# z of a forgetting-attention layer: from inside the attention loop to a stage of its own, by seven half-size products

## The chip, the cores and the metric

One core of one Trainium2 chip runs the whole step. The metric is device time in microseconds of one execution; the time of a kernel is the median of its runs.

## What is computed

Two layers over 640 tokens: 512 of a prompt and 8 x 16 new ones ("samples"), width 1024, inner width 2048. Layer 0 is a gated MLP, layer 1 an attention with 16 heads of 128 in which each head's output is gated:

```python
proj = h @ w_in                              # layer 1: q, k, v, z, each 2048 wide, and 16 forget logits
s = einsum(q, k) * scale + c_i - c_j         # c: running sum of log_sigmoid(forget logit)
p = softmax(where(key <= query, s, -inf))    # prompt: 512 keys; samples: 256 cached and 16 new keys
out = (einsum(p, v) * silu(z)) @ w_out
```

Both layers end with a norm, a residual and a gated per-layer embedding (the "tail"). k, v and the log forget values are outputs too. All data is fp32.

## The kernel before

A product in fp32 accuracy is made of three matmuls (`mm3`): each operand is split into a rounded part and a rest (`split`: ScalarE writes the rounded part, VectorE the rest), and high x high, high x rest, rest x high add up in one PSUM bank. So every weight is fetched (`fetch`, DMAs issued by SP, 512 KB a unit, into three or four buffers `RAW`), split into the ring `W` (`prefetch`), and used by `weights(n)`. Units come in the order of the list `units`. The activations `h` of all 640 tokens lie split in `A` (`h_hi`, `h_lo`).

Layer 0 makes its two gates u and z by `seven_products`: a 256-channel by 1024 by 640-token product is cut in two along each axis, and seven half-size products (four steps of 128 x 128 x 320 columns by `mm3`, 84 matmuls) take the place of eight (96 matmuls of 384 or 256 columns in layer 1). It costs sums: of the weights on GpSimd (`left_operands`, four of 512 elements a pair), of the activations once on VectorE (`right_operands`), and seven additions out of PSUM a pair on VectorE.

Layer 1 works on pairs of heads. `project(p, parts)` makes v, k, q and z of pair p, as generators that yield after each few matmuls how long they took (in nominal steps). `interleave(steps, pieces)` runs these steps and calls pieces of the attention of the pair before at given times: `prompt_pieces` (scores, `turn`, that is, transposes of the probabilities, and value products, four blocks a head) and `sample_pieces`. So TensorE's long projections cover the softmax on VectorE and ScalarE. The loop runs p = 0 to 6: project pair p + 1, attend pair p. At p = 6, z of pair 7 is left out of the loop and made after it, and the attention of pair 7 lies beside that z and the first output products of the `tail`. y of each pair goes to DRAM (`y_sc`) and is read back in the tail.

The order within an engine is set by the tile framework: it takes the program as written and re-orders the instructions of each engine by its own timeline. Each engine then runs its list in order; all DMAs but one are issued by SP, one after the other.

Of the kernel before, what the change touches and what calls it, by code (L numbers as in the profile page):

```python
# [56 lines left out]
def hybrid_trunk(tc, x_prompt, x_sample, ck, cv, clf, p_prompt, p_sample, norm_pre, norm_post,  # L58
# [27 lines left out]
    c_sc = dram.tile([H, SEQ], F32, name="c_sc")  # L86
    cs_sc = dram.tile([P, 272], F32, name="cs_sc")
    rs_sc = dram.tile([16, P], F32, name="rs_sc")

    def r1(o, n, p=P):  # L90
        return R1[:p, o:o + n]
# [62 lines left out]
    for p in range(8):  # L154
        for part in (2, 1, 0, 3):
            for kk in range(2):
                u_rows(f_win[0], kk * 512, part * E + p * 256, 4, 256)
    u_tail(f_wout, 1)
# [3 lines left out]
    S0, S1 = 16, 48  # L162
    SEVEN = (0, 2)
    items = []
    for i in range(len(units)):
        if not S0 <= i < S1 or i % 4 - i % 2 not in SEVEN:
            items.append((i, None))
        elif i % 2 == 0:
            items += [(i, j) for j in range(4)]

    n0 = S1 + 16 + 2 + 8
    few = range(n0, n0 + 64 + 12)
    place, last_use = [], [-1] * (2 * NW)
    state = {"raw": 0, "used": 0}

    def raw_of(i):
        if S0 <= i < S1:
            z = (i - S0 + 1) % 4
            if z == NRAW:
                return r1(o_X, 1024)  # L180
        else:
            z = i % NRAW if i < S0 else (i + 1) % NRAW
        return RAW[:, z * 1024:z * 1024 + 1024]
# [7 lines left out]
    def left_operands(i, j):  # L191

        (a11, a21), (a12, a22) = ([raw_of(r).rearrange("p (k n) -> p k n", k=4)[:, :, z:z + P] for z in (0, P)] for r in (i, i + 1))
        s2, s3, s1, s4 = (SF[:, z * 512:z * 512 + 512].rearrange("p (k n) -> p k n", k=4) for z in range(4))
        if j == 0:
            for o, a, b, op in ((s1, a21, a22, ALU.add), (s2, s1, a11, ALU.subtract), (s3, a11, a21, ALU.subtract),
                                (s4, a12, s2, ALU.subtract)):
                nc.gpsimd.tensor_tensor(out=o, in0=a, in1=b, op=op)
        return (a11, SF[:, :1024], SF[:, 1024:2048], raw_of(i + 1))[j]

    def prefetch(upto, i0=0):

        while len(place) < min(upto, len(items)):
# [13 lines left out]
            if j is None:  # L217
                split(hi, lo, raw_of(u))
            else:
                split(*((x.rearrange("p (k n) -> p k n", k=4) for x in (hi, lo)) if j == 0 else (hi, lo)), left_operands(u, j))  # L220
                if u > S0:
                    fetch(u + 4)
# [84 lines left out]
    def channel_steps(ws, hh, banks, splits=SPLITS):  # L307

        out = [bank(banks), bank(banks)]
        for k in range(8):  # L310
            w = [z[:, k % 4, hh * P:(hh + 1) * P] for z in ws[k // 4]]
            for (a, b), o in zip(splits, out):
                mm3(o[:, :b - a], w, h_at(k, a, b), k == 0, k == 7)
            yield 0.9
        return out
# [69 lines left out]
    o_X, o_ln, o_sum, o_th = 14208, 15232, 16256, 17216  # L385
# [4 lines left out]
    SF = pool2.tile([P, 2560], F32, name="sf")  # L390

# [6 lines left out]
    b11, b12, b21, b22, t_a, t_b = (r1(10240 + z * 1280, 1280).rearrange("p (k n) -> p k n", k=4) for z in (0, 1, 2, 3, 4, 0))  # L398

    def right_operands():  # L400

# [3 lines left out]
        for o, a, b, dst in ((t_a, b12, b11, 0), (t_b, b22, t_a, 1), (b21, b21, t_b, 2), (b12, b22, b12, None)):  # L405
            nc.vector.tensor_tensor(out=o, in0=a, in1=b, op=ALU.subtract)
            if dst is not None:
                split(*right_sum(dst), o)

# [24 lines left out]
    for p in range(4):  # L434
# [4 lines left out]
        for kk in range(4):  # L439
# [20 lines left out]
    fetch(S0 + 4)  # L460
# [25 lines left out]
    assert o_A + 256 <= o_X  # L486
# [63 lines left out]

    def eight_products(done):
        wz = weights(2)
        for i in range(2):
            for j, o in enumerate(channel_unit(wz, i, UZ)):
                done(i, j, o[:, :HT])
# [32 lines left out]
    for g in range(0, 16, 2):  # L588
        for part, finish in ((0, finish_u), (1, finish_z)):
            if 2 * part in SEVEN:  # L590
                seven_products(lambda i, j: uv_of(g + i)[part][:, HALF[j]], lambda i, j, c: finish(g, i, j, c))
            else:
                eight_products(lambda i, j, c: finish(g, i, j, c))
# [138 lines left out]
    pool2, R2 = second("r2b", F32)  # L732


    o = 0
    def tmpa(n, p=P):
        nonlocal o
        res = r2(o, n, p)
        o += n
        return res  # L740
# [22 lines left out]
    assert o <= 7168  # L763
# [314 lines left out]
    def y_again(g, half):  # L1078
# [3 lines left out]
        if half == 0 and 7 <= g < 11:  # L1082
            return f(A[:, 7680 + (g - 7) * TOK:7680 + (g - 6) * TOK])
        return r1(g * TOK, TOK) if g < 7 else r2((g - 7) * TOK, TOK)
# [5 lines left out]
    PARTS = (project_v, project_k, project_q, project_z)  # L1090
    interleave(project(0, PARTS), [(0.0, forget_logits), (6.0, log_forget), (20.0, forget_sums), (30.0, lambda: load_k(0, 0))])
    for p in range(7):
        length, step = (57, 5.6) if p < 6 else (43, 4.2)
        pieces = kv_times(p, 0, 5) + kv_times(p, 1, length / 2) + sample_times(p, 0, 5) + sample_times(p, 1, length / 2)
        pieces += [(2, lambda p=p: load_k(p, 1)), (length / 2 - 3, lambda p=p: load_k(p + 1, 0))]
        for hh in range(2):
            pieces += prompt_times(2 * p + hh, 2 + 4 * step * hh, step)
        interleave(project(p + 1, PARTS if p < 6 else PARTS[:3]), pieces)
        store_y(p)


# [43 lines left out]
```

## Time and profile before

| | |
|---|---|
| runs | 1334.85, 1336.32, 1334.9 us; median 1334.9 |
| profiled execution | 1334.83 us, span 1333.0 us |
| TensorE matmul busy | 1321.0 us (99% of the span) |
| VectorE, ScalarE, GpSimd busy | 766.4, 542.9, 135.7 us |
| granted TensorE clock, mean | 0.999 |
| DMA | 172.87 MB, 130 GB/s over the span |

Matmuls are pipelined: a matmul of 320 columns is shown as 310 ns, but the next one starts about 147 ns later. So what one costs is read from start to start, and a stretch of TensorE from the first start of one part to the first start of the next. `L249` to `L251` are the three lines of `mm3`, `L263` and `L264` the two of `split`, `L198` the weight sums, `L528` the additions of the seven products, `L583` a gate product, `L960` value products, `L953` transposes of probabilities, `L955` their copy out of PSUM, `L992` the transposes of the cached keys, `L406` a sum of `right_operands`. PE is TensorE, DVE VectorE, ACT ScalarE, POOL GpSimd.

### The profile page before, as it was taken

How to read it: one execution, taken by the hardware profiler on the slowest of the kernel's cores; microseconds unless marked ns; L12 is line 12 of the kernel's file. 1: busy time of each engine (PE TensorE's matmuls, PEld its weight loads, DVE VectorE, ACT ScalarE, POOL GpSimd, SP SyncE). 2: the span in 40 equal slices, each digit the busy share in tenths (PEclk: the TensorE clock that was granted, in tenths of full speed). 3: DMA queues.
4: the chain of work that ended last, by engine and by line, in shares of the span. 5: the costliest groups of instructions: out<-in, count | busy, mean ns of one | idle time of the engine just before them, and what ended most of it. 6: DMA issues, size and time to landing. Idle time of an engine off the chain costs nothing.

```text
span 1333.0 us, 21550 instructions
## 1 busy us (share of the span) xinstructions
PE 1321.0 (99%) x8363; PEld 1191.6 (89%) x8363; DVE 766.4 (57%) x1581; ACT 542.9 (41%) x1025; POOL 135.7 (10%) x144
## 2 busy tenths in 40 slices
PE   9999999999999999999999999999999999999998
PEld 6888999999988788999999999999999998888786
DVE  7744899998844546544545454444545465544642
ACT  5434555444535334523433333433334344435341
POOL 1013444543000100000000000000000000000100
PEclk9999999999999999999999999999999999999999
DMA  6432334232324204688778575778778687243211
GB/s 224 138 100 70 120 114 130 66 109 68 127 95 158 78 18 127 178 142 158 138 154 176 145 163 141 164 144 163 125 151 169 152 212 235 101 149 111 64 64 47
DMA packets 299913, 172.87 MB, mean 130 GB/s; under 512 B 188769, under 2 KB 269201, under 8 KB 299810
## 3 DMA queue, kind: packets, MB, share of 16 engines
q1 hardware_dynamic: 299666, 171.23, 51.7%
q8 instruction: 65, 1.06, 0.3%
q14 instruction: 38, 0.31, 0.1%
q10 hardware_dynamic: 144, 0.26, 0.1%
HBM read 149.86 MB, written 21.59 MB: 129 GB/s over the span
## 4 chain that ended last, share of the span: by engine, by line
PE 94%; DVE 3%; issue 1%; ACT 1%; DMA 0%; POOL 0%; SPq 0%; DVEq 0%
PE pb L249 28%; PE pb L251 27%; PE pb L250 27%; PE pb L960 3%; PE pb L953 1%; PE pb L1014 1%; PE pb L1040 1%; PE pb L287 1%; DVE W L264 1%; PE pb L565 1%; PE pb L1037 1%; DVE R L583 0%; DMA RAW<-in_gmlp_w_in 0%; PE pb L1032 0%; DVE R L528 0%
## 5 line engine op out<-in xcount | busy, mean ns | idle before, releaser
L249 PE MATMUL pb<-A,W 128*128 128x384 f32 (+2 forms) x1024 | 330.2, 322 | 2.1 <-DVE R L538 1.8
L251 PE MATMUL pb<-A,W 128*128 128x384 f32 (+2 forms) x1024 | 317.1, 310 | 0.0
L250 PE MATMUL pb<-A,W 128*128 128x384 f32 (+2 forms) x1024 | 316.6, 309 | 0.0
L249 PE MATMUL pb<-W,A 128*128 128x512 f32 (+1 forms) x840 | 298.3, 355 | 2.1 <-ACT R L686 1.4
L251 PE MATMUL pb<-W,A 128*128 128x512 f32 (+1 forms) x840 | 293.7, 351 | 0.6 <-DVE A L264 0.6
L250 PE MATMUL pb<-W,A 128*128 128x512 f32 (+1 forms) x840 | 294.0, 350 | 0.0
L264 DVE TENSOR_TENSOR W<-RAW,W 128x1024 fp32r<-128x1024 f32 (+1 forms) x156 | 194.0, 1244 | 139.7 <-ACT W L263 137.5
L263 ACT ACTIVATE W<-RAW 128x1024 fp32r<-128x1024 f32 (+1 forms) x156 | 161.1, 1033 | 156.8 <-PE pb L250 65.1
L249 PEld LDWEIGHTS pb<-A,W 128*128 128x128 f32 x1024 | 193.0, 188 | 10.9 <-issue 6.8
L250 PEld LDWEIGHTS pb<-A,W 128*128 128x128 f32 x1024 | 193.0, 189 | 0.6
L251 PEld LDWEIGHTS pb<-A,W 128*128 128x128 f32 x1024 | 192.6, 188 | 0.4 <-issue 0.4
L249 PEld LDWEIGHTS pb<-W,A 128*128 128x128 f32 x840 | 159.1, 189 | 26.4 <-issue 3.1
L251 PEld LDWEIGHTS pb<-W,A 128*128 128x128 f32 x840 | 158.9, 189 | 21.1 <-DVE A L264 0.9
L250 PEld LDWEIGHTS pb<-W,A 128*128 128x128 f32 x840 | 159.0, 189 | 20.4 <-issue 0.4
L264 DVE TENSOR_TENSOR A<-R,A 128x640 fp32r<-128x640 f32 (+1 forms) x51 | 41.0, 835 | 74.1 <-ACT A L263 71.9
L992 DVE STREAM_TRANSPOSE r2b_t<-r2b_t 128x256 f32<-128x256 f32 x128 | 46.4, 413 | 33.9 <-PE pb L1014 26.2
L263 ACT ACTIVATE A<-R 128x640 fp32r<-128x640 f32 (+1 forms) x51 | 36.6, 746 | 67.7 <-PE pb L250 65.7
L249 PE MATMUL pb<-tb,W 128*128 128x320 f32 x192 | 59.8, 312 | 0.1
L251 PE MATMUL pb<-tb,W 128*128 128x320 f32 x192 | 59.5, 310 | 0.0
L250 PE MATMUL pb<-tb,W 128*128 128x320 f32 x192 | 59.5, 310 | 0.0
L273 POOL TENSOR_TENSOR SML<-SML 128x1 f32<-128x1 f32 x25 | 18.1, 724 | 385.1 <-DVE SML L271 380.5
L955 ACT ACTIVATE R<-pb 128x128 f32<-128x128 f32 (+1 forms) x64 | 27.9, 436 | 65.7 <-PE pb L953 65.4
(235 smaller groups left out, 1866.7 us busy)
## 6 DMA issues: line engine op xcount, KB each, us to landing
RAW<-in_fox_w_in SPq DMA_DIRECT2D x64, 512.0 KB
RAW<-in_gmlp_w_in SPq DMA_DIRECT2D x40, 512.0 KB
r2b_t<-in_cache_fox_v SPq DMA_DIRECT2D x32, 512.0 KB
r2b_t<-in_cache_fox_k SPq DMA_DIRECT2D x128, 128.0 KB
RAW<-in_gmlp_w_out SPq DMA_DIRECT2D x16, 512.0 KB
RAW<-in_ple_w_gate SPq DMA_DIRECT2D x16, 512.0 KB
RAW<-in_fox_w_out SPq DMA_DIRECT2D x16, 512.0 KB
out<-R SPq DMA_DIRECT2D x40, 128.0 KB
```

What stands on the lines that cost most here:

```text
L249: nc.tensor.matmul(out, lh, rh, start=start, stop=False)
L250: nc.tensor.matmul(out, lh, rl, start=False, stop=False)
L251: nc.tensor.matmul(out, ll, rh, start=False, stop=stop)
L263: nc.scalar.activation(out=hi, in_=src, func=AF.Copy)
L264: nc.vector.tensor_tensor(out=lo, in0=src, in1=f(hi), op=ALU.subtract)
L273: nc.gpsimd.tensor_tensor(out=q, in0=t, in1=mhalf, op=ALU.pow)
L287: nc.tensor.transpose(out=b[:, j * P:(j + 1) * P], in_=src[:, (4 * c + j) * P:(4 * c + j + 1) * P], identity=ident)
L565: nc.tensor.matmul(b0[:, t * P:(t + 1) * P], v_at(pnl, t)[:, c0:c0 + P], wm, start=True, stop=True)
L953: nc.tensor.transpose(out=tb[:, j * P:(j + 1) * P], in_=pr[:, j * P:(j + 1) * P], identity=ident)
L955: nc.scalar.activation(out=pt[:, :n], in_=tb[:, :n], func=AF.Copy)
L960: nc.tensor.matmul(O[:, d], v[:, j, hh * P:(hh + 1) * P], pt[:, j * P:(j + 1) * P], start=(j == 0), stop=(j == i))
L992: nc.vector.transpose(out=kt[:, hh, bl, :PAST], in_=kr[:, hh, bl])
```

## The change

z of all eight pairs is made ahead of the loop by `seven_products`, and goes to DRAM (`z_sc`); each pair's z is read back in the pass that needs it. For this, v and k of pair 0 are projected first, then the right operands are made (beside them), then z of pairs 0 to 7, then q of pair 0. The loop's passes project v, k and q only, and are 43 steps long instead of 57, with the same attention in them. In pass 0 the samples come later (12 and 27 steps instead of 5 and 28.5) so that the prompt blocks stand ahead of them; pass 6 has blocks 3.4 steps apart instead of 4.2 and stores and reloads y at its end. The attention of pair 7 now lies beside the tail alone. The third factor of the seven (`t3`) and its buffers become arguments, the weight sums of layer 1 lie in `R1`, a fourth raw buffer serves the new stage, and the small tiles of the forget sums move from the second pool to `R1`, since the right operands take that pool until the stage ends.

```diff
+    u_pair(0, (2, 1))
+    Z0 = len(units)
+    for p in range(8):
+        u_pair(p, (3,))
+    Z1 = len(units)
+    u_pair(0, (0,))
+    for p in range(1, 8):
+        u_pair(p, (2, 1, 0))
...
-    SEVEN = (0, 2)
+    SEVEN = ((16, 48, 14208), (Z0, Z1, 13504))
...
-    few = range(n0, n0 + 64 + 12)
+    few = range(Z1, n1 + 12)
...
-    pool2, R2 = second("r2b", F32)
+    pool2, TB = second("r2k", F32R)
+    state["sums"] = r1(10496, 2048)
...
-    def project_z(p):
-        ws = weights(2)
-        for hh in range(2):
-            tz = z_of(2 * p + hh)
-            banks = yield from channel_steps(ws, hh, PRJ)
-            for (a, b), ps in zip(SPLITS, banks):
-                nc.scalar.activation(out=tz[:, a:b], in_=ps[:, :b - a], func=AF.Tanh, scale=0.5)
-                nc.vector.scalar_tensor_tensor(out=tz[:, a:b], in0=tz[:, a:b], scalar=1.0, in1=ps[:, :b - a], op0=ALU.add, op1=ALU.mult)
+    def make_z(p):
+        zst = r1(4608 + (p % 2) * 2 * TOK, 2 * TOK)
+        def into(i, j):
+            return zst[:, i * TOK:(i + 1) * TOK][:, HALF[j]]
+        def done(i, j, c):
+            th = r1(14528 + j * HT, HT)
+            nc.scalar.activation(out=th, in_=c, func=AF.Tanh, scale=0.5)
+            nc.vector.scalar_tensor_tensor(out=into(i, j), in0=th, scalar=1.0, in1=c, op0=ALU.add, op1=ALU.mult)
+        seven_products(into, done, right_sum(3), 12544)
+        dma(z_sc[2 * p:2 * p + 2].rearrange("h p t -> p h t"), zst.rearrange("p (h t) -> p h t", h=2))
+    def z_again(p):
+        dma(r1(RA + (p % 2) * 4608 + 3328, 2 * TOK).rearrange("p (h t) -> p h t", h=2), z_sc[2 * p:2 * p + 2].rearrange("h p t -> p h t"))
...
-    PARTS = (project_v, project_k, project_q, project_z)
-    interleave(project(0, PARTS), [(0.0, forget_logits), (6.0, log_forget), (20.0, forget_sums), (30.0, lambda: load_k(0, 0))])
+    PARTS = (project_v, project_k, project_q)
+    interleave(project(0, PARTS[:2]), [(3.0, forget_logits), (9.0, log_forget), (9.5, lambda: right_operands(12544, 3)), (26.0, forget_sums)])
+    for p in range(8):
+        make_z(p)
+    pool2.release()
+    pool2, R2 = second("r2b", F32)
+    run(project_q(0))
+    length = 43
     for p in range(7):
-        length, step = (57, 5.6) if p < 6 else (43, 4.2)
+        t0, t1 = (12, 27) if p == 0 else (5, length / 2)
+        step = 4.2 if p < 6 else 3.4
+        pieces = [(t0 - 14, lambda p=p: z_again(p))]
...
-    interleave(project_z(7), [x for x in pieces if x[0] <= now])
-    tail(1, y_again, (0, 1, 2, 3, 4), [(t - now, g) for t, g in pieces if t > now])
+    tail(1, y_again, (0, 1, 2, 3, 4), pieces)
```

Three places in the order of instructions, each as it stands before and now.

First, VectorE as layer 1 starts. `A<-pb` are the splits of the last token tiles, `W<-RAW` those of weights, `WF` the forget weights; lines 781 to 793 of the old file work on the forget logits, 867 to 870 on k of pair 0. Before:

```order
L264 TENSOR_TENSOR A<-pb_77,A 128x4x128
L264 TENSOR_TENSOR A<-pb_75,A 128x4x128
L264 TENSOR_TENSOR W<-RAW,W 128x1024
L781 COPY r2b_t<-pb_76 128x160
L782 TENSOR_TENSOR r2b_t<-r2b_t 128x80
L264 TENSOR_TENSOR W<-RAW,W 128x1024
L783 TENSOR_TENSOR r2b_t<-r2b_t 128x80
L785 SCALAR_TENSOR_TENSOR r2b_t<-r2b_t 128x80
L787 TENSOR_SCALAR r2b_t<-r2b_t 128x80
L789 SCALAR_TENSOR_TENSOR r2b_t<-r2b_t 128x80
```

Now, with lines 417 and 419 the sums and differences of the right operands, `r2k_t` their splits, and `W<-R_69` the splits of weight sums of z:

```order
L279 TENSOR_TENSOR A<-pb_75,A 128x4x128
L417 TENSOR_TENSOR R_69<-A 128x1280 x2
L419 TENSOR_TENSOR R_69<-R_69 128x1280 x2
L279 TENSOR_TENSOR r2k_t<-R_69,r2k_t 128x1280
L419 TENSOR_TENSOR R_69<-R_69 128x1280
L279 TENSOR_TENSOR W<-R_69,W 128x1024
L787 COPY R_69<-pb_76 128x160
L279 TENSOR_TENSOR r2k_t<-R_69,r2k_t 128x1280
L419 TENSOR_TENSOR R_69<-R_69 128x1280
L279 TENSOR_TENSOR W<-R_69,W 128x1024
L788 TENSOR_TENSOR R_69<-R_69 128x80
L279 TENSOR_TENSOR r2k_t<-R_69,r2k_t 128x1280
```

Between the last token tile and the first products of z there now stand eight operations of 1280 elements and four splits of the same size, with the forget logits and k in between.

Second, SP's queue after the forget sums (`c_sc`, `cs_sc`) have gone to DRAM. Before, cached keys, one unit of weights and the masks of the attention follow:

```order
L119 DMA c_sc<-r2b_t 16x512
L119 DMA cs_sc<-r2b_t 128x272
L119 DMA out<-R_69 32x4x32
L119 DMA r2b_t<-in_cache_fox_k 32x32x32 x4
L119 DMA RAW<-in_fox_w_in 128x4x256
L119 DMA r2b_t<-c_sc 128x512
L119 DMA R_69<-cs_sc 128x1x272
L119 DMA r2b_t<-in_cache_fox_k 32x32x32 x4
```

Now z of pairs 0 and 1 is stored and read again, with units of z weights between:

```order
L121 DMA c_sc<-R_69 16x512
L121 DMA cs_sc<-R_69 128x272
L121 DMA z_sc<-R_69 128x2x640
L121 DMA R_69<-z_sc 128x2x640
L121 DMA RAW<-in_fox_w_in 128x4x256 x2
L121 DMA z_sc<-R_69 128x2x640
L121 DMA R_69<-z_sc 128x2x640
L121 DMA R_69<-in_fox_w_in 128x4x256
L121 DMA RAW<-in_fox_w_in 128x4x256
```

The reading of z of a pair stands directly behind its storing, and weights of later pairs behind both; the cached keys stand behind the stage.

Third, TensorE near the end of the attention of the last head (`pb_70` to `pb_74` are the first half of the output products, `pb_75` in its first rows below the second half). Before, the transposes of the last block (line 953) and its value products (line 960) stand 22 output products apart, of which the first are:

```order
L251 MATMUL pb_70<-W,A 128x512
L960 MATMUL pb_77<-R_69 128x128 x3
L953 MATMUL pb_76<-CST,r2b_t 128x128 x4
L249 MATMUL pb_70<-W,A 128x512
L250 MATMUL pb_70<-W,A 128x512
L251 MATMUL pb_70<-W,A 128x512
L249 MATMUL pb_71<-W,A 128x512
L250 MATMUL pb_71<-W,A 128x512
```

Now, with line 975 the value products and line 968 the transposes:

```order
L266 MATMUL pb_74<-W,A 128x512
L975 MATMUL pb_77<-R_69 128x128 x2
L264 MATMUL pb_76<-W 128x512
L265 MATMUL pb_76<-W 128x512
L266 MATMUL pb_76<-W 128x512
L968 MATMUL pb_75<-CST,R_69 128x128 x3
L975 MATMUL pb_77<-R_69 128x128 x3
L264 MATMUL pb_75<-W,A 128x512
L265 MATMUL pb_75<-W,A 128x512
L266 MATMUL pb_75<-W,A 128x512
```

The transposes of block 2 are followed at once by its value products; 15 matmuls of the second half later, the transposes and value products of block 3 stand in the same way.

More of the change, by code (lines that the diff above doesn't have):

```diff
@@ L86, in hybrid_trunk @@
     c_sc = dram.tile([H, SEQ], F32, name="c_sc")
+    z_sc = dram.tile([H, P, TOK], F32, name="z_sc")
     cs_sc = dram.tile([P, 272], F32, name="cs_sc")
@@ L153, in hybrid_trunk, with u_pair @@
     u_tail(g_wout, 0)
-    for p in range(8):
-        for part in (2, 1, 0, 3):
+    def u_pair(p, parts):
+        for part in parts:
             for kk in range(2):
                 u_rows(f_win[0], kk * 512, part * E + p * 256, 4, 256)
+    u_pair(0, (2, 1))
[6 more added lines that the diff above has]
+        u_pair(p, (2, 1, 0))
+    n1 = len(units)
     u_tail(f_wout, 1)
-    S0, S1 = 16, 48
-    SEVEN = (0, 2)
+    SEVEN = ((16, 48, 14208), (Z0, Z1, 13504))
     items = []
+    raw_slot, raw_last = [], [-1] * (NRAW + 1)
+    part_of = {}
     for i in range(len(units)):
-        if not S0 <= i < S1 or i % 4 - i % 2 not in SEVEN:
+        part = next((x for x in SEVEN if x[0] <= i < x[1]), None)
+        if part is None:
             items.append((i, None))
-        elif i % 2 == 0:
+        elif i % 2 == part[0] % 2:
             items += [(i, j) for j in range(4)]
-    n0 = S1 + 16 + 2 + 8
-    few = range(n0, n0 + 64 + 12)
+            part_of[i] = part
+        if part and i == part[0]:
+            raw_last[NRAW] = i
+        z = min(range(NRAW + (part is not None)), key=lambda z: raw_last[z])
+        raw_last[z] = i
+        raw_slot.append(RAW[:, z * 1024:z * 1024 + 1024] if z < NRAW else r1(part[2], 1024))
+    few = range(Z1, n1 + 12)
     place, last_use = [], [-1] * (2 * NW)
-    state = {"raw": 0, "used": 0}
+    state = {"raw": 0, "used": 0, "sums": None}
     def raw_of(i):
[L177 to L183, printed above, removed]
+        return raw_slot[i]
     def fetch(upto):
@@ L193, in left_operands @@
         (a11, a21), (a12, a22) = ([raw_of(r).rearrange("p (k n) -> p k n", k=4)[:, :, z:z + P] for z in (0, P)] for r in (i, i + 1))
-        s2, s3, s1, s4 = (SF[:, z * 512:z * 512 + 512].rearrange("p (k n) -> p k n", k=4) for z in range(4))
+        sf = state["sums"]
+        s2, s3, s1, s4 = (sf[:, z * 512:z * 512 + 512].rearrange("p (k n) -> p k n", k=4) for z in range(4))
         if j == 0:
@@ L305, in hybrid_trunk, with channel_steps @@
     SPLITS = ((0, SA), (SA, TOK))
-    def channel_steps(ws, hh, banks, splits=SPLITS):
+    def channel_steps(ws, hh, banks):
         out = [bank(banks), bank(banks)]
@@ L311, in channel_steps @@
             w = [z[:, k % 4, hh * P:(hh + 1) * P] for z in ws[k // 4]]
-            for (a, b), o in zip(splits, out):
+            for (a, b), o in zip(SPLITS, out):
                 mm3(o[:, :b - a], w, h_at(k, a, b), k == 0, k == 7)
@@ L390, in hybrid_trunk @@
     SF = pool2.tile([P, 2560], F32, name="sf")
+    state["sums"] = SF[:, :2048]
     def quarter(i, j):
@@ L396, in right_sum, with right_operands @@
         return tuple(TB[:, z:z + 4 * HT].rearrange("p (k n) -> p k n", k=4) for z in (i * 2560, i * 2560 + 1280))
[L398 to L400 removed]
+    def right_operands(base, t3):
+        b11, b12, b21, b22 = (r1(base + z * 1280, 1280).rearrange("p (k n) -> p k n", k=4) for z in range(4))
         for q, (i, j) in zip((b11, b12, b21, b22), ((0, 0), (0, 1), (1, 0), (1, 1))):
@@ L549, in seven_products @@
                 total(1, 0, u3, o)
[L551 to L555, printed above, removed]
     def gate_spatial(g):
@@ L589, in hybrid_trunk @@
         for part, finish in ((0, finish_u), (1, finish_z)):
[L590 to L593, printed above, removed]
+            seven_products(lambda i, j: uv_of(g + i)[part][:, HALF[j]], lambda i, j, c: finish(g, i, j, c), quarter(0, 1), o_sum)
         if g < 6:
@@ L1081, in y_again @@
             return y_of(g)
-        if half == 0 and 7 <= g < 11:
-            return f(A[:, 7680 + (g - 7) * TOK:7680 + (g - 6) * TOK])
-        return r1(g * TOK, TOK) if g < 7 else r2((g - 7) * TOK, TOK)
+        if g < 7:
+            return r1(g * TOK, TOK)
+        if g >= 11:
+            return r2((g - 11) * TOK, TOK)
+        return f(A[:, 7680 + (g - 7) * TOK:7680 + (g - 6) * TOK]) if half == 0 else r2((g - 4) * TOK, TOK)
     def load_y(heads, half):
```

49 lines of the change are left out of this document (26 added, 23 removed).

## The prediction

> **What bounds the kernel now.** I read the page first, then busy time by stretches, then the matmuls in order of time, and last the groups by form. On the page, one execution:
>
> ```profile
> span 1333.0 us, 21550 instructions
> PE 1321.0 (99%) x8363; PEld 1191.6 (89%) x8363; DVE 766.4 (57%) x1581; ACT 542.9 (41%) x1025; POOL 135.7 (10%) x144
> DVE  7744899998844546544545454444545465544642
> DMA  6432334232324204688778575778778687243211
> PE 94%; DVE 3%; issue 1%; ACT 1%; DMA 0%; POOL 0%; SPq 0%; DVEq 0%
> ```
>
> The chain that ended last is 94% TensorE; everything else is followed back to matmuls. DVE is near full in one place only, slices 5 to 9 (the gated branch of layer 0, where the seven products already run); the DMA engines are busiest in the attention loop, slices 16 to 33. The profiled execution took 1334.83 us, 1.8 above its span, and the median of the three runs is 1334.9: the sum below is made against 1334.8 and needs no correction for that.
>
> Busy time by stretches: I cut at the first matmul of each part (z of pair 0, then seven passes of the loop, then the start of the tail). The columns are length, then busy time and count for each engine, granted clock, DMA share, GB/s.
>
> ```profile
> core 0: us, PE busy (x) PEld busy (x) DVE busy (x) ACT busy (x) POOL busy (x), PEclk, DMA share, GB/s
> 126.88:347.59 220.71, 218.46 (x1519) 216.69 (x1518) 202.01 (x309) 114.87 (x212) 91.90 (x58) 1.00 0.33 101
> 560.27:592.09 31.82, 31.82 (x209) 29.93 (x207) 16.54 (x36) 10.83 (x18) 1.72 (x3) 1.00 0.79 139
> 592.09:606.27 14.18, 14.18 (x98) 14.18 (x97) 3.54 (x5) 4.71 (x8) 0.22 (x1) 1.00 0.96 163
> 606.27:680.15 73.88, 73.88 (x570) 70.25 (x569) 36.04 (x110) 27.37 (x62) 1.51 (x6) 1.00 0.80 158
> ...
> 975.70:1049.59 73.89, 73.89 (x571) 70.25 (x569) 36.04 (x110) 27.19 (x62) 1.39 (x6) 1.00 0.72 152
> 1049.59:1109.15 59.56, 59.56 (x474) 55.88 (x473) 32.50 (x104) 24.98 (x57) 2.15 (x6) 1.00 0.82 193
> 1109.15:1188.35 79.20, 79.20 (x465) 65.77 (x463) 43.79 (x110) 33.65 (x65) 0.47 (x2) 1.00 0.46 153
> ```
>
> Two things stand here. From z of pair 0 to the end of the attention TensorE is never idle, and the clock is full. And the seventh pass of the loop (1049.59 on) is already what the changed loop is to be in every pass: v, k and q of one pair, no z, beside one pair's attention with blocks 4.2 steps apart. It takes 59.56 us against 73.88, and TensorE does not wait in it. The difference, 14.32, is z of one pair and nothing else.
>
> **What the change removes.** z of pair 0 takes 14.18 us with nothing beside it; z in six passes takes 6 x 14.32 = 85.9; z of pair 7 stands in the last stretch among the last pair's attention and I take 14.18 for it too. Together 114.3 us, all of it on the path.
>
> **What it adds on TensorE.** Eight times seven products. One such run, of layer 0, with nothing between its 84 matmuls:
>
> ```profile
> 139.62 0.31 PE L249 MATMUL pb<-A,W 128*128 128x320 f32 x1
> 151.79 0.31 PE L251 MATMUL pb<-tb,W 128*128 128x320 f32 x1
> ```
>
> From the first start to the last, plus one more interval (83 intervals in 12.17, so 0.147 each), is 12.32 us; eight are 98.6, the lower end. Upper end: the whole stage of layer 0 (126.88 to 347.59) holds sixteen such runs in 220.71 us. Sixteen clean ones are 197.1; of the other 23.6 the spatial matmuls below take 17.5, and 6.1 are left, 0.38 a run. Eight runs at 12.70 are 101.6. I take 100.0, nearer the lower end because part of the 6.1 is transposes and sample products that the new stage lacks. **Net on TensorE: 114.3 - 100.0 = 14.3 us less** (15.7 to 12.7).
>
> **Can the other engines feed it?** Groups by form, and for the last six rows minimum, median and maximum of one instruction:
>
> ```profile
> L264 DVE TENSOR_TENSOR W<-RAW,W 128x1024 fp32r<-128x1024 f32 x148 | 187.5, 1268 | 139.7 <-ACT W L263 137.5 <-DMA out<-R 0.5
> L264 DVE TENSOR_TENSOR W<-sf,W 128x1024 fp32r<-128x1024 f32 x32 | 39.1, 1222 | 11.6 <-ACT W L263 11.6
> L264 DVE TENSOR_TENSOR W<-R,W 128x512 fp32r<-128x512 f32 x40 | 28.3, 709 | 0.7 <-ACT W L263 0.7
> L528 DVE TENSOR_TENSOR R<-R,pb 128x320 f32<-128x320 f32 x64 | 29.5, 477 | 0.4
> L565 PE MATMUL pb<-R 128*128 128x128 f32 x128 | 17.5, 275 | 0.0
> L264 DVE TENSOR_TENSOR tb<-R,tb 128x1280 fp32r<-128x1280 f32 x3 | 4.4, 1482 | 0.0
> L583 DVE SCALAR_TENSOR_TENSOR R<-sf,R x16: 477/798/1589, 148.3 to 351.4; 128x320 f32<-128x320 f32 x16
> L583 DVE SCALAR_TENSOR_TENSOR R<-R x16: 477/488/1586, 153.7 to 353.8; 128x320 f32<-128x320 f32 x16
> L198 POOL TENSOR_TENSOR sf<-RAW x16: 1282/1472/1810, 86.3 to 305.2; 128x512 f32<-128x512 f32 x16
> L198 POOL TENSOR_TENSOR sf<-RAW,sf x16: 1276/2158/2382, 98.0 to 318.9; 128x512 f32<-128x512 f32 x16
> L198 POOL TENSOR_TENSOR sf<-sf,RAW x8: 1282/1298/2224, 96.6 to 306.6; 128x512 f32<-128x512 f32 x8
> L406 DVE TENSOR_TENSOR R<-R x4: 1481/1482/1483, 53.3 to 60.1; 128x1280 f32<-128x1280 f32 x4
> ```
>
> DVE for one pair: weight splits 0.709 + 2 x 1.222 + 1.268 = 4.42; seven adds out of PSUM at 0.477 = 3.34; four gate products at 0.488 = 1.95. Sum 9.7 us of the 12.3 that TensorE takes. In layer 0 it did 202.01 / 16 = 12.6 in 13.8 and TensorE stayed busy. POOL does two sums like 1.472, one like 1.298, one like 2.158: 6.4 us. The two splits of the sums must wait for it and it for them, but that ring is the same in layer 0. No cost beyond the 100.0.
>
> A rule against the change: the SBUF lesson of the Trainium skill (SBUF — State Buffer, Who interferes with whom) says that a VectorE instruction with two SBUF inputs and a GpSimd instruction that reads SBUF shut each other out for their whole length. The row agrees in part: L583 takes 477 ns at best and up to 1589, and POOL's third sum 1276 at best and 2158 in the middle. By that rule the stage would go by the first rival below, not by 100.0.
>
> **New waits.** *Start of the stage.* The right operands are now made while v and k of pair 0 run: eight adds and subtracts of 1280 at 1.482 (L406) and four splits at 1.482 (the tb row), 17.8 us more on DVE. The last token tile is there at
>
> ```profile
> 551.17 1.29 DVE L264 TENSOR_TENSOR A<-pb,A 128x512 fp32r<-128x512 f32 x2 [3.26 <-ACT A L263]
> 567.66 3.07 SPq L119 DMA_DIRECT2D r2b_t<-in_cache_fox_k  x4
> 574.18 0.45 DVE L992 STREAM_TRANSPOSE r2b_t<-r2b_t 128x256 f32<-128x256 f32 x1 [3.81 <-DMA r2b_t<-in_cache_fox_k]
> ```
>
> so about 552.5; k of pair 0 ends where z begins less one q, 592.09 - 14.2 = 577.9. That leaves 25.4 us. DVE was busy 16.54 of 31.82 us there, 13.2 in 25.4; with 17.8 it is 31.0, some 5.6 too much. But the cache transposes and q's copies move behind the stage, and the order of DVE puts only two right operands ahead of the first three products. Between 0 and 5.6 I take 1.0.
>
> *Through DRAM.* Eight stores of 640 KB and eight loads. In SP's new order the loads of pair 0 and 1 stand right behind their stores, ahead of weights, and wait for the landing. No row times a store followed by its load; the nearest is above, four cache loads issued from 567.66 and their first reader released at 574.18: 6.5 us. The weights queued behind are those of later pairs, so one pair's 12.3 us cover it: nothing; without cover 2 x 6.5. Later loads stand far from their stores.
>
> *First pair.* The cache tiles share memory with the right operands, so their loads start only when the stage ends. q takes 14.2 us and the samples come 12 steps later; the loads need 6.5 for four. 0.5, between 0 and 3.
>
> *Passes 0 to 5.* As the old seventh pass: nothing. Bytes: 152 GB/s x 73.89 = 11.2 MB, less 1.05 of weights, plus 0.66 of z, is 10.8 in 59.56 us, 182 GB/s; the old seventh pass moved 193 without a wait.
>
> *The end.* The last pair had 14 steps of z beside it and now has not. In the new order the transposes of the last two blocks are followed at once by their value products (the third place above), where 22 matmuls stood between. Each time TensorE waits for the copy out of PSUM:
>
> ```profile
> L955 ACT ACTIVATE R<-pb 128x512 f32<-128x512 f32 x16 | 9.5, 597 | 49.7 <-PE pb L953 49.7
> L955 ACT ACTIVATE R<-pb 128x384 f32<-128x384 f32 x16 | 7.8, 490 | 1.3 <-PE pb L953 1.2
> L944 ACT ACTIVATE r2b_t<-r2b_t,SML 128x512 f32<-128x512 f32 x11 | 8.0, 723 | 9.5 <-DVE SML L943 9.5
> L962 DVE SCALAR_TENSOR_TENSOR R<-pb,R 128x512 f32<-128x512 f32 x16 | 10.8, 676 | 23.8 <-PE pb L960 23.8
> L263 ACT ACTIVATE A<-R 128x640 fp32r<-128x640 f32 x50 | 35.4, 736 | 62.2 <-PE pb L250 60.2 <-issue 1.5 <-PE pb L251 0.5
> L264 DVE TENSOR_TENSOR A<-R,A 128x640 fp32r<-128x640 f32 x50 | 39.5, 821 | 68.6 <-ACT A L263 66.4 <-PE pb L251 1.5 <-PE pb L250 0.7
> ```
>
> 0.6 and 0.5 with about 0.4 around each, say 2.0; the softmax of the last block (0.72 for the exponential and its neighbours) has 15 matmuls beside it, 1.0 more. The gate and split of the last head (0.68 + 0.74 + 0.82) lie beside 26 matmuls of the second half: nothing. 3.0, between 0 and 6.
>
> **Sum.** -14.3 + 1.0 + 0.5 + 3.0 = -9.8: 1334.8 - 9.8 = **1325.0 us**.
>
> **Rivals.** *Vector and GpSimd take turns:* DVE's two-SBUF work (4.42 + 1.95) and POOL's 6.4 make 12.8 a pair, the stage 102.4; 1327.4. For it L583's long ones; against it layer 0, where DVE's and POOL's time (202.0 + 91.9) exceed the stage's 220.7, so much lies side by side. *All covered:* 98.6 and no new wait, 15.7 less: 1319.1. For it: TensorE does not idle anywhere in this stretch now. *The seams eat it:* start 5.6, first pair 3, DRAM 6.5 once, in total 15.1 with none at the end, against 14.3: about 1335.6, no change. *Slower, by the DMA queues in the shorter passes:* the share of 0.80 in the second row of the loop is 59 us of DMA time, and a pass is to take 59.56. If that time does not shrink and no pass can run above the 0.82 of the old seventh, a pass takes 72, 12.5 more, six times 75, less 9.8: 1400. It decides from 1.6 us a pass (9.8 / 6). Against it: the seventh pass carries the same cache rows, and DMA time there fell to 0.82 x 59.56 = 49 us.
>
> **Chances.** The forecast 0.58 (own range 1322 to 1329), taking turns 0.12, all covered 0.15, seams 0.08, slower 0.07. A difference of 0.2% (2.7 us) is what a measurement can tell. Faster: 0.85; same 0.08; slower 0.07. The range, 1319.5 to 1331.5, leaves out the two last and the far ends.
>
> **What would show it.** Eight runs of 84 matmuls at 12.3 to 12.7 us each between k and q of pair 0; DVE busy 75 to 90% there; six passes of 59.6 (61 or more would speak for the queues, seen as TensorE waiting for splits behind loads of weights or cache transposes); a gap of a few us on TensorE before the first product, and about 1 us twice before the last value products (L975 of the new file). A pair at 12.8 or more with POOL's sums near 2 us each would show turns taken. Wrong altogether if a pass of the loop is much above 60.

## The result: 0.42% slower, and the profile after

The changed kernel takes 1341.1 us in the median (1334.3 to 1344.4, 20 runs), the kernel before 1334.9 (1334.0 to 1336.6, 20 runs). The ratio is 1.0042, 95% interval 1.0031 to 1.0052. The forecast was 1325.0 (1319.5 to 1331.5), a gain: the sign was wrong. Single executions of the changed kernel lie up to 10 us apart, those of the kernel before 2.6. One execution of a later experiment (first keys loaded during the stage) took 2155 us at a mean granted clock of 0.56, where the others had 0.99 or more, and is left out of that experiment's numbers.

The profiled execution took 1338.6 us, 2.1 of it outside the span. From its page (span; busy time; DVE, granted clock and DMA in 40 slices; the chain that ended last by engine):

```profile
span 1336.4 us, 21600 instructions
PE 1313.4 (98%) x8267; PEld 1180.0 (88%) x8267; DVE 844.3 (63%) x1665; ACT 564.0 (42%) x1053; POOL 185.9 (14%) x176
DVE  7755899998844546799865554655555563544642
PEclk9999999999999999999999999999999998999999
DMA  6432344232424204456498789998878898443111
PE 87%; DVE 5%; DMA 4%; issue 1%; ACT 1%; SPq 1%; POOL 0%; DVEq 0%; ACTq 0%
```

TensorE is busy for 7.6 us less (1321.0 to 1313.4), yet the span is 3.4 us longer. The chain is 87% TensorE where it was 94%, with 4% DMA and 5% VectorE: TensorE waits for something now. Busy time by stretches says where; I cut at the first matmul of the stage, of its second run, of q of pair 0, of passes 0, 1, 2 and 6, and at the end of pass 6:

```profile
576.87:593.00 16.13, 15.36 (x97) 13.27 (x96) 15.12 (x24) 9.52 (x14) 9.46 (x6) 1.00 0.65 112
593.00:679.37 86.37, 86.37 (x590) 86.24 (x589) 78.22 (x109) 39.23 (x63) 33.65 (x22) 1.00 0.59 157
693.67:754.52 60.85, 60.16 (x475) 56.03 (x473) 33.65 (x106) 24.58 (x57) 1.11 (x5) 1.00 0.88 166
754.52:819.00 64.48, 61.75 (x476) 57.66 (x473) 32.80 (x106) 23.37 (x56) 1.33 (x6) 0.97 0.87 185
819.00:1057.58 238.58, 238.58 (x1891) 223.86 (x1890) 129.99 (x416) 95.66 (x220) 5.58 (x24) 1.00 0.87 180
1057.58:1117.80 60.22, 60.22 (x480) 56.48 (x481) 34.41 (x107) 24.38 (x56) 3.16 (x7) 1.00 0.95 238
1117.80:1336.40 218.60, 207.29 (x988) 165.32 (x984) 104.00 (x198) 83.04 (x149) 4.92 (x7) 0.98 0.33 107
```

Seven runs of seven products in 86.37 us are 12.34 each, with TensorE never idle and DVE at 91%: the stage is as forecast. Four passes in 238.58 are 59.64 each: as forecast too. The losses are at the seams, where one part of the program hands over to the next. Before the change the same parts were 67.57 (project of pair 0, 538.70 to 606.27, q and z included), 6 x 73.88, 59.56 and 223.85, so by place, in the profiled execution:

| place | forecast by its terms | measured | over |
|---|---|---|---|
| pair 0 and the stage (to the end of q) | 100.0 - 14.18 + 1.0 = +86.8 | 155.78 - 67.57 = +88.2 | +1.4 |
| passes 0 to 5 | -85.9 + 0.5 = -85.4 | 363.9 - 443.3 = -79.4 | +6.0 |
| pass 6 | 0 | 60.22 - 59.56 | +0.7 |
| the tail | -14.2 + 3.0 = -11.2 | 218.6 - 223.85 = -5.2 | +6.0 |

Together +4.3; less 0.8 us that the part ahead of the change was shorter, that is the 3.4 us between the spans. This execution is 2.5 us below the median of the changed kernel, so the table covers 3.8 of the 6.2 us between the medians.

Now the waits. A wait is counted here from the start of the last matmul ahead of it to the start of the next one; the profile's own rows of idle time, which begin at the modelled end of a matmul, show 0.3 to 0.4 us less. *Forget logits*, the chain in order of time (start, length, what):

```profile
547.91 3.71 DMA x_sc<-R
...
551.76 3.56 DMA R<-in_fox_w_in
...
556.67 0.36 PE pb L777
```

The raw forget weights now lie in R1 at 4608, in the place of the last tile of x1, and can be loaded only when its store has landed; TensorE stands from 554.1 to 556.7. *Pass 1*, from its chain:

```profile
765.87 10.23 DMA RAW<-in_fox_w_in
...
787.89 3.37 DMA r2b_t<-in_cache_fox_k
...
792.25 0.33 DVE R L1032
792.64 0.38 PE pb L264
```

There are gaps of 0.9 and 2.4 us. The first is followed back to a load of weights that took 10.23 us to land, and to its splits on DVE. The longer one stands behind the samples' maximum on DVE (L1032), which stands behind the transposes of a cached block that landed only at 791.3. A stretch of half clock behind it costs 1.7 us more (last section). *The start of the tail*, first the queue of SyncE:

```profile
1106.88 6.92 SPq L121 DMA_DIRECT2D out<-R  x8
1113.89 0.95 SPq L121 DMA_DIRECT2D r2b_t<-in_cache_fox_v  x2
1115.04 0.83 SPq L121 DMA_DIRECT2D R<-in_p_prompt  x2
1115.92 0.90 SPq L121 DMA_DIRECT2D R<-y_sc  x2
```

and the chain from there:

```profile
1115.92 5.51 DMA R<-y_sc
1121.46 0.74 ACT A L278
1122.25 0.80 PE pb L264
```

Heads 0 and 1 of y lie where v of pair 6 lies, so they can be loaded only after the last value products of that pair, and they stand in SyncE's order behind eight stores of k and a load of `in_p_prompt` that waits for one of these stores to land (1112.8 to 1115.0); they land 5.5 us after their issue. In the kernel before, 14 us of z of pair 7 lay over this. Now TensorE waits 4.3 us, and then works at half clock for 6.8 us (the rows stand in the last section). *The end*: 0.8, 0.9 and 1.0 us ahead of the last products of the last pair, 2.7 against a forecast of 3.0.

My theory after this reading: the saving on TensorE came as forecast and was spent at seams where z had covered loads. Rivals: the DMA queues are too full in the shorter passes generally; or the added traffic of z through DRAM is the cause. The experiments are changes of the changed kernel; "after" is its median of 1341.1. From the experiment with GpSimd's queue on, the runs are from other chips, on which the kernel before took 1335.1 and 1335.5 us and the changed kernel itself was not run; gains of 3 us against "after" are weak evidence there.

### The profile page after: what moved, and what is told of

Same layout as the page of the kernel before. It is cut to its first block, busy times and chain, and to the rows that moved or that the text cites. A ratio compares the mean times of both kernels' runs of the same rounds, so it can differ in the third digit from the quotient of the medians.

```text
span 1336.4 us, 21600 instructions
## 1 busy us (share of the span) xinstructions
PE 1313.4 (98%) x8267; PEld 1180.0 (88%) x8267; DVE 844.3 (63%) x1665; ACT 564.0 (42%) x1053; POOL 185.9 (14%) x176
## 4 chain that ended last, share of the span: by engine, by line
PE 87%; DVE 5%; DMA 4%; issue 1%; ACT 1%; SPq 1%; POOL 0%; DVEq 0%; ACTq 0%
PE pb L264 26%; PE pb L266 25%; PE pb L265 25%; PE pb L975 2%; DVE W L279 2%; DMA RAW<-in_fox_w_in 2%; PE pb L302 1%; PE pb L1029 1%; PE pb L968 1%; PE pb L1055 1%; PE pb L573 1%; SPq L121 1%; DMA R<-cs_sc 0%; ACT W L278 0%; PE pb L1052 0%
## 5 line engine op out<-in xcount | busy, mean ns | idle before, releaser
L264 PE MATMUL pb<-A,W 128*128 128x384 f32 (+2 forms) x864 | 277.9, 322 | 2.5 <-DVE R L552 2.0
L266 PE MATMUL pb<-A,W 128*128 128x384 f32 (+2 forms) x864 | 268.1, 310 | 0.0
L265 PE MATMUL pb<-A,W 128*128 128x384 f32 (+2 forms) x864 | 267.6, 310 | 0.0
L278 ACT ACTIVATE W<-RAW 128x1024 fp32r<-128x1024 f32 (+1 forms) x154 | 156.2, 1015 | 133.0 <-PE pb L266 54.3
L264 PEld LDWEIGHTS pb<-A,W 128*128 128x128 f32 x864 | 163.0, 189 | 10.5 <-issue 5.9
L265 PEld LDWEIGHTS pb<-A,W 128*128 128x128 f32 x864 | 163.1, 189 | 0.6
L266 PEld LDWEIGHTS pb<-A,W 128*128 128x128 f32 x864 | 162.8, 188 | 0.1
L278 ACT ACTIVATE A<-R 128x640 fp32r<-128x640 f32 (+1 forms) x51 | 36.3, 745 | 81.9 <-PE pb L265 63.5
L279 DVE TENSOR_TENSOR W<-R,W 128x512 fp32r<-128x512 f32 (+1 forms) x58 | 51.1, 889 | 6.1 <-ACT W L278 6.1
```

The costliest lines, as they stand in the source:

```text
L264: nc.tensor.matmul(out, lh, rh, start=start, stop=False)
L265: nc.tensor.matmul(out, lh, rl, start=False, stop=False)
L266: nc.tensor.matmul(out, ll, rh, start=False, stop=stop)
L278: nc.scalar.activation(out=hi, in_=src, func=AF.Copy)
L279: nc.vector.tensor_tensor(out=lo, in0=src, in1=f(hi), op=ALU.subtract)
```

## The experiments

**Again.** No edit.

> The changed kernel itself, unchanged, for a second profile and for its spread. If the waits at the seams are waits for transfers (the theory that the saving of TensorE came and was spent where z used to cover loads), the six seven-product runs stay at 12.3 us each and passes 2 to 5 at 59.6, while pass 0, pass 1 and the start of the tail differ from the first profile by some us: 1334 to 1345 us in all. If the DMA queues are short in every pass (the rival), passes 2 to 5 vary too, by 1 us or more each.

1341.9 us (1337.9 to 1343.9). Runs in the stage 12.32, passes 2 to 5 59.65 again; passes 0 and 1 took 60.7 and 66.7, the wait at the tail 3.3. In all fourteen traces with the stage, passes 2 to 5 take 59.65 each (one pass of one trace 59.81). So the steady passes have no shortage and the seams vary.

**Other heads first in the tail.**

```
- load_y(range(7), 0)
+ load_y((2, 3, 4, 5, 0, 1, 6), 0)      # products and rows of w_out in the same order
```

> The tail of layer 1 takes its first heads in the order 2, 3, 4, 5, 0, 1, 6 in place of 0 to 6, so that its first products need no head that lies where the last pass's values lay. By the theory of the seams the gap of 4.3 us at the start of the tail goes, and the halved clock behind it (6.8 us, about 3.4 us of work lost) with it: 7 to 8 us less than the changed kernel, about 1333 us. If the halved clock has another cause than the gap, it stays, and only 4.3 us are won. If the queues are short there in any order (the DMA share is 0.95 to 0.97), the wait moves to a later head and under 2 us are won.

1338.4 us, ratio to before 1.0024 (1.0012 to 1.0037): 2.7 won where my theory said 7 to 8, and the interval still overlaps that of the changed kernel. The first products no longer wait, but a later head does: a gap of 3.0 us at 1123.8, and the half clock again. Reordering alone does not bring y earlier; my theory was too narrow here.

**Pair 0's cached keys left out.**

```
  kr, _, _ = kv_of(p, bg)
+ if p == 0:
+     nc.gpsimd.memset(kr, 0.0)
+     return
```

> The cached keys of pair 0 of layer 1 are not loaded; GpSimd fills their place with zeros, so the outputs of layer 1 differ and 1 MB or so of transfers is left out. By the theory of the seams passes 0 and 1 lose their gaps (60.9 and 64.5 us before) and take 59.6 each, with no halved clock in pass 1: 6 us less, about 1335 us; the start of the tail stays. If the passes are short of transfers in general, pass 1 keeps 62 us or more, since its own loads are as before.

1331.6 us, 0.9975 (0.9963 to 0.9987): 9.5 won, more than forecast. Passes 0 and 1 are clean, the wait at the tail stays (4.0 us):

```profile
696.52:756.23 59.71, 59.71 (x474) 56.03 (x473) 31.00 (x101) 24.82 (x57) 1.33 (x6) 1.00 0.73 126
756.23:815.87 59.64, 59.64 (x476) 55.96 (x474) 32.87 (x106) 23.84 (x56) 1.11 (x5) 1.00 0.86 185
```

**Forget weights to a free place.**

```
- wf_raw = tmpa(128).rearrange(...)
+ wf_raw = r1(16896, 128).rearrange(...)
```

> The raw forget weights of layer 1 are loaded into a place of R1 that nothing reads or writes at that time, in place of the one that the store of x must leave first. By the theory of the seams the gap of 2.5 us ahead of the forget logits goes: about 2.5 us less, 1338.5 us. If the logits wait for something else as well (the conversion on VectorE, or the key of the queue), the gap shrinks by under 1 us, and the time stays at 1341.

1338.5 us, 1.0032 (1.0020 to 1.0045): 2.6 won, as forecast, but the interval overlaps that of the changed kernel, so by the time alone the gain is not sure. The logits' gap is not in this trace; part of it comes back at the forget sums, where TensorE idles 1.6 us in place of 0.6.

**z of pair 7 beside the tail again.**

```
- for p in range(8): make_z(p)
+ for p in range(7): make_z(p)
+ interleave(project_z(7), ...)          # ahead of the tail, as before the change
```

> One part of the change is undone: the stage makes z of pairs 0 to 6 only, and z of pair 7 is made with three products beside the first part of the tail, as in the kernel before. It costs 14.2 us of TensorE in place of 12.3, so 1.9 more. By the theory of the seams the wait at the start of the tail (4.3 us and the halved clock behind it, some 7.5 us in all) and the three waits among the last value products (2.6 us) go: 8 us less than the changed kernel, about 1333 us, with pass 0 and pass 1 as long as there. If the queues are simply full at the end (the rival), the wait comes back at the next heads of the tail, and the time is 1340 or above.

1330.0 us, 0.9959 (0.9944 to 0.9975): 11.1 won over four executions, 8 expected. Passes 0 and 1 keep 60.7 and 63.5, as expected. Neither the wait at the start of the tail nor the three at the end are left.

**No trip through DRAM.**

```
- dma(z_sc[...], zst)
- dma(r1(...), z_sc[...])
+ nc.gpsimd.memset(r1(...), 1.0)
```

> z is neither stored to DRAM nor loaded from it; GpSimd fills its place with ones, so the outputs of layer 1 differ, and 10.5 MB of transfers are left out. By the theory of the seams the trip has little to do with the loss: pass 0 and pass 1 stay above 60 and 62 us, the wait at the start of the tail stays above 3 us, 1 to 2 us less in all, 1339 to 1340 us. If the added traffic is what fills the queues (the rival), these waits all but vanish: 10 us less or more, 1331 us or below.

1333.0 us, 0.9989 (0.9980 to 0.9998): 8 won, between the two forecasts and nearer to the rival's. The wait at the tail is gone, pass 1 takes 59.63, pass 0 still 60.71. In this trace the forget logits start 5.0 us later than in the changed kernel's (561.68 against 556.67; why stays open), and from pass 0 to the end it is 11.2 us shorter: behind the stage the rival's forecast is met. So the trip is part of the cause at the seams, which my theory had denied.

**First keys loaded during the stage.**

```
- kr = r2(o_K, 2048)
+ kr = (r2(o_K, 2048) if i else r1(7168, 2048))      # load_k(0, 0) ahead of make_z(3)
- pieces.append((0, lambda: load_k(0, 0)))
+ pieces.append((0, lambda: load_k(0, 1)))
```

> The first block of pair 0's cached keys is loaded during the stage, into columns of R1 that are free there (1 MB in 128-byte pieces), and the second block at the end of the stage, in place of both behind the stage. Nothing is left out. By the theory of the seams pass 0 and pass 1 come to within 1 us of 59.6 each: 5 to 8 us less than the changed kernel, about 1334 us, most of what leaving these keys out gave (1331.6). If it was the amount of transfers and not their place, the backlog only moves, and under 2 us are won.

1332.5 us (median of nine; the tenth is the one of 2155 us), 0.9982 (0.9966 to 0.9997), 8.6 won with nothing left out. The second block now takes the first one's place behind the stage. Passes 0 and 1 take 59.70 and 60.58. So at that seam another place of the load is enough, with the amount the same.

**Three repairs together** (forget weights, first keys, z of pair 7).

> Three repairs together: the forget weights loaded to a free place, the first block of pair 0's cached keys loaded during the stage, and z of pair 7 made beside the tail. By the theory of the seams the gains add: 2.5, 5 to 8 and 8 us off the changed kernel's 1341, so 1323 to 1326 us, below the kernel before (1334.5) by 9 to 11 us, which is about the saving that the TensorE sum gave. If the losses share one cause, such as the queues or the halved clock alone, the gains overlap, and it stays near 1331.

1324.6 us (1324.2 to 1325.3), ratio 0.9925 (0.9912 to 0.9938): faster than the kernel before by 9.9 us. That is 16.5 below the changed kernel, within the 15 to 18 expected; by themselves the three won 2.6 + 8.6 + 11.1 = 22.3, so they overlap by a quarter. Passes 0 and 1:

```profile
682.00:741.70 59.70, 59.70 (x474) 56.02 (x473) 30.91 (x101) 24.55 (x57) 1.25 (x6) 1.00 0.83 181
741.70:801.34 59.64, 59.64 (x476) 55.96 (x474) 32.88 (x106) 23.84 (x56) 1.19 (x6) 1.00 0.87 185
```

and all that TensorE waits for from pass 0 to the end (line, releaser: total, times, longest):

```profile
PE pb L264 <- ACT R L691: 0.7, 1, 0.7
```

The DMA share is hardly lower than in the changed kernel (0.88 and 0.87). It is not the fullness of the engines in a steady pass that cost the time, but what is due right behind a seam.

**The z loads on GpSimd's queue.**

```
- dma(r1(...), z_sc[...])                # SyncE
+ nc.gpsimd.dma_start(out=r1(...), in_=z_sc[...])
```

> Each pair's z comes back from DRAM by GpSimd's queue in place of SyncE's: the same bytes, at their own time, with nothing of the other loads standing behind them. The kernel without the trip lost its waits in pass 1 and at the start of the tail (1333.0). If that was the order in SyncE's queue (the z load waits for its place to come free, and the rest stands behind), these waits go here too: about 1333 us. If it was the bytes, which the full DMA engines must move in any case, pass 1 stays above 61 us and the wait at the start of the tail above 2.5 us: 1339 to 1342 us.

1332.4 us, 0.9982 (0.9973 to 0.9991): 8.7 won, the time that the order in the queue would give. The trace is divided: the wait at the tail shrinks from 4.3 to 1.0 us with no half clock, as by the order; passes 0 and 1 keep 61.57 and 63.89, as by the bytes. On GpSimd the eight loads waited 18.5 us for their places (L977 is the gate product on VectorE, which reads the z that lay there) and 7.3 for the stores:

```profile
L909 POOL DMA_DIRECT2D R<-z_sc x8: 722/724/867, 602.0 to 1059.1; - x8
  DVE R L977: 18.5, 4
  DMA z_sc<-R: 7.3, 2
```

In the changed kernel, where they stand later in SyncE's order, the eight took 6.4 us of it, the longest 2.36. Without them SyncE came to heads 0 and 1 of y at 1112.68 in place of 1115.92. What TensorE waits for at the start of the tail:

```profile
PE pb L264 <- ACT A L278: 0.6, 1, 0.6
```

**Work in place of the wait.**

```
+ b = bank(PRJ)
+ for i in range(36):
+     nc.tensor.matmul(b[:, :256], WF[:, :P], WF, start=True, stop=True)
```

> 36 matmuls of the forget weights with themselves, whose result nobody reads, stand ahead of the first product of the tail: 36 x 0.118 = 4.2 us of TensorE work in the place of the wait of 4.3 us. If the halved clock behind that wait comes from TensorE's idling, it does not come here, and 3.4 us are won (6.8 us at half speed): 1337 to 1338 us. If it comes from something else (the place in the program, a load on the chip), it stays, and the time is 1341 or, where the wait is short, up to 4 us more.

1336.8 us, 1.0016 (1.0007 to 1.0025): 4.3 won by adding 4.2 us of useless work to TensorE, 3.4 expected. As the time is from another chip, and the next experiment wins 3.3 there with the same passes, the trace is the better evidence. The 36 matmuls (shortest, median, longest in ns; first and last start):

```profile
L1135 PE MATMUL pb<-WF x36: 280/283/287, 1117.9 to 1122.1; 128*128 128x256 f32 x36
```

After them the clock stays whole (the third column from the end; in this trace a half clock of 3.4 us stands only behind the wait for the forget logits):

```profile
1122.00:1125.40 3.40, 2.86 (x13) 1.22 (x16) 2.90 (x4) 3.32 (x6) 0.00 (x0) 1.00 1.04 411
1125.40:1128.80 3.40, 2.30 (x20) 1.04 (x18) 3.04 (x8) 0.63 (x2) 1.27 (x2) 1.00 1.04 405
```

**The first pair's samples at their usual place.**

```
- t0, t1 = (12, 27) if p == 0 else (5, length / 2)
+ t0, t1 = 5, length / 2
```

> The other part of the change is undone: in pass 0 the sample blocks of pair 0 stand where those of the other pairs do (steps 5 and 21.5), not at 12 and 27. By the theory of the seams the cached keys, which can be loaded only behind the stage, are then awaited by TensorE in pass 0: 3 to 6 us longer there, part of it won back in pass 1 since the loads are no later; 1342 to 1346 us. If the place of the samples does not matter (the loads of the next pairs are what is late), it stays at 1341 within 1.

1337.8 us, 1.0016 (1.0001 to 1.0032), no slower and rather 3.3 faster than after: a miss. Passes 0 and 1 took 62.3 and 62.8, in sum 125.1 against 125.3. Pass 0 loses what pass 1 gains; the amount to be loaded behind the stage is the same in either order. In the passes this part of the change neither helps nor is the cause. Where the 3.3 us come from is open; this trace has one stretch of half clock, that of the changed kernel three.

**A fourth repair: the forget sums later.**

```
- (26.0, forget_sums)
+ if p == 2: forget_sums()               # behind make_z(2); ex made in log_forget
```

> The three repairs that gave 1324.6, and a fourth: the forget sums stand behind the stage's third pair, and the product that they need is made ahead of the right operands on VectorE (five small tiles lie elsewhere for it). By the theory of the seams the two waits at the start of the stage (1.3 and 1.9 us) go: about 3 us less, 1321.5 us, with the first run of seven products at 12.3 to 12.8 us in place of 18.0. If VectorE is behind there for another reason (the right operands alone fill it), the waits move to the first products of the stage, and it stays at 1324.

1324.6 us, 0.9919 (0.9905 to 0.9932): no gain. The first run takes 14.3 us in place of 18.0, but the second 14.2, and the sums with their neighbours 2.6 behind the third. The waits moved, as the rival said:

```profile
PE pb L264 <- DVE R L542: 1.6, 1, 1.6
PE pb L264 <- DVE R L883: 1.0, 1, 1.0
```

VectorE is behind there by some 3 us, through the right operands and the pieces put beside them.

**All eight pairs in the stage, with the other repairs.** z loads on GpSimd's queue, first keys during the stage, forget weights moved, and the last pair's blocks closer:

```
- pieces += prompt_times(14 + hh, 4 + 21 * hh, 5.2)
+ pieces += prompt_times(14 + hh, 4 + 17 * hh, 4.2)
```

> All eight pairs' z in the stage, as in the changed kernel, and no z beside the tail; z comes back by GpSimd's queue, the first block of pair 0's keys is loaded during the stage, the forget weights go to a free place, and the blocks of the last pair stand 4.2 steps apart in place of 5.2. If the losses were four places with four causes (the order in SyncE's queue at the start of the tail, the keys in passes 0 and 1, the place of the forget weights, the copies before the last value products), passes 0 and 1 take 59.7 each, the wait at the start of the tail is 1 us or less, and the time is 1321 to 1324 us, no more than with z of pair 7 beside the tail (1324.6), since that costs 1.9 us of TensorE. If the tail needs z of pair 7 as cover whatever the queues do, its wait is 3 us or more again, with a halved clock, and the time is 1326 to 1330.

1331.1 us (1329.4 to 1334.9), 0.9968 (0.9957 to 0.9979): faster than before, but 6.5 above the version with z of pair 7 beside the tail (5.7 by the ratios, since the chips differ). Passes 0 and 1 take 59.71 and 59.63, so the early keys clear them. The tail waits 2.2 us again, with a half clock of 3.4, and the last products still 0.85 and 0.96 us (pass 1, then TensorE's waits around the start of the tail and the last pair):

```profile
757.96:817.59 59.63, 59.63 (x475) 55.95 (x474) 32.89 (x106) 23.70 (x56) 2.05 (x7) 1.00 0.89 191
```

```profile
PE pb L264 <- ACT A L278: 1.8, 1, 1.8
PE pb L975 <- ACT R L970: 1.3, 2, 0.7
```

The time lies above both forecasts and the wait between them, nearer to the second: the queue shortens the wait, and of the kernels that keep the trip only those with z of pair 7 as cover are without it. In the profiled execution, the slowest of the seven, the stage also took 106.1 us (577.84 to 683.95) in place of 102.5, with single runs of seven products up to 13.1 behind the first; why, with these edits together, stays open, as does the share of the z loads' bytes and of their order in passes 0 and 1.

## Why the prediction was wrong, by its own steps

- **What it removes and adds on TensorE: right.** Seven runs of 12.3 to 12.5 us each; the first took 16.1 with the forget sums inside. That TensorE is busy for 7.6 us less, and not 14.3, is in part the half clock: three stretches of 3.41 us at half speed are 5.1 us more busy time (an estimate), and with them out it is 12.7, the low end of the range. The first and the last matmul of one run:

```profile
593.00 0.31 PE L264 MATMUL pb<-A,W 128*128 128x320 f32 x1
605.17 0.31 PE L266 MATMUL pb<-r2k_t,W 128*128 128x320 f32 x1
```

  What the Trainium skill says on turns (SBUF — State Buffer, Who interferes with whom) did not set the time here: DVE was at 91% (75 to 90 forecast) beside GpSimd's 33.65 us and no run was longer than 12.5. The rival of 12.8 a pair falls. But these runs could not have shown turns by their time: GpSimd had run ahead and made 20 of the 32 sums in them, 4.8 us a run, and with DVE's 6.4 that is 11.2 even in turns. GpSimd's sums again took 1.30 to 2.17 us, so the lengthening is there, with room for it.
- **Passes 0 to 5 as the old seventh: right for four of six.** 59.64 against 59.56 at a DMA share of 0.87. The rival of 72 us a pass falls.
- **"First pair", 0.5 (0 to 3): the first step that failed.** Passes 0 and 1 together lost 6.0 us (1.2 and 4.8). I sized it by four loads alone, 6.5 us. But both blocks of keys, the values, the weights and the keys of the next pair come due at once behind the stage, and the backlog reaches into pass 1. Left out or loaded early, these keys win 9.5 and 8.6 us over ten and nine executions.
- **"The end", 3.0: right for the last products (2.7), and it left out the start of the tail.** I asked what z of pair 7 covers among the last pair's attention, not what else it covered: the reload of heads 0 and 1. No term stood for it. It cost 4.3 us and a half clock, some 6 in all; with z of pair 7 back, 11.1 us over four executions (with the 2.7).
- **"Through DRAM", 0: failed by its question.** I priced the trip's landing, and saw no weights late. What counted was what else moves at these seams: without the trip 8 us were won, and 8.7 with the z loads on a queue of their own. How much of it is their place in SyncE's order and how much their bytes stays open. The range named there (2 x 6.5) would have held it.
- **"Start of the stage", 1.0 (0 to 5.6): mis-sized within its range.** VectorE is some 3 us behind; and the forget weights' new place, 2.6, was not seen: the text on it costed what moved on DVE, not what the new address waits for.
- **"The seams eat it", 0.08, was the rival that came nearest**, with a price of 15.1 us for all seams; found were 18.6, the 4.5 forecast and 14.1 more (1.4 + 6.0 + 0.7 + 6.0). It had the right kind of cause at two of its three places. It deserved more, since the terms at 0 to 1.0 were taken at or near the lower end of their ranges all at once. The sum on TensorE itself was sound: with three repairs, and seven pairs in the stage, its terms give 12.6 us less (114.3 - 14.2 - 7/8 of 100.0), and TensorE is busy for 12.5 less (1321.0 to 1308.5). That the time is then 1324.6, so near to 1325.0, is partly luck, as it is another kernel with other waits.

## What to carry to other kernels

When work is taken out of a loop, list every transfer that it covered, at the first and the last iteration above all; the steady iterations can be exactly as planned and the gain still be gone at the seams. Price a moved buffer by what its new address must wait for, and a load put into an in-order queue by what stands behind it, not by its own landing alone. Here a wide run-to-run spread where there was little (10 us against 2.6, and 1.1 after the repairs) came with the waits for transfers and went with them.

## What the hardware showed beyond this

Short waits of TensorE halved its clock. Stretches of 3.41 us, cut where the clock changed, of the kernel after (the third column from the end is the granted clock):

```profile
554.87:558.28 3.41, 1.61 (x10) 0.95 (x11) 2.31 (x5) 1.28 (x3) 1.59 (x2) 1.00 0.73 130
558.28:561.69 3.41, 3.41 (x28) 2.74 (x27) 3.41 (x4) 0.48 (x1) 0.00 (x0) 1.00 0.41 94
790.39:793.80 3.41, 1.34 (x10) 1.16 (x9) 2.09 (x9) 0.20 (x1) 0.40 (x2) 1.00 0.85 199
793.80:797.21 3.41, 3.41 (x17) 3.41 (x17) 2.29 (x8) 1.52 (x4) 0.00 (x0) 0.50 0.84 230
1118.07:1121.48 3.41, 0.25 (x6) 0.00 (x0) 0.00 (x0) 0.02 (x1) 0.00 (x0) 1.00 0.93 249
1121.48:1124.89 3.41, 2.64 (x5) 1.14 (x6) 2.67 (x4) 3.41 (x6) 0.24 (x1) 0.50 1.03 410
1124.89:1128.30 3.41, 3.41 (x9) 2.64 (x9) 3.28 (x10) 0.77 (x3) 0.46 (x1) 0.50 1.04 404
```

The half clock comes in whole stretches of 3.413 us, one or two at a time, and the two places of this trace start 327.68 us apart, 96.0 such stretches: the grid runs by itself. A stretch in which TensorE was busy for 1.34 or 0.25 us is followed by half clock, one with 1.61 is not. In layer 1 of all the traces the stretches ahead of the start of a half clock have 1.66 us or less, and all but that one of the others 1.68 or more. The same wait of 2.55 us ahead of the forget logits was not followed by it here, and was in the second run of the same kernel, where the grid fell otherwise:

```profile
553.72:557.13 3.41, 1.19 (x8) 0.79 (x7) 0.55 (x2) 1.07 (x3) 2.95 (x3) 1.00 0.73 97
557.13:560.54 3.41, 3.41 (x13) 1.61 (x12) 3.23 (x5) 0.21 (x1) 0.00 (x0) 0.50 0.68 147
```

So a wait of somewhat over 2 us can cost up to 1.7 us more (3.41 at half speed), by chance of its place. Behind waits of 3.0 to 5.8 us, in eight traces, the half clock lasted one stretch three times and two stretches five times; what decides that is open, as TensorE worked for 1.2 us or more of the first. The Trainium skill (TensorE: Matmul & The Clock Gate, Part 1) has the free-running window of 3413 ns, and the traces agree; its limit of idle gaps of some 3.4 us (same page, HAM oscillation) is longer than the waits of 2.1 to 2.6 us (1.8 to 2.3 idle) that were enough in six traces here.
